# MLP up-projection by tokens with 512-wide moving weights, its inner layer turned by VectorE and through HBM

## The chip, the core and the metric

The kernel runs on one core of a Trainium2 chip. Five engines matter: TensorE (PE in the profile; PEld is its load of the still operand), VectorE (DVE), ScalarE (ACT), GpSimd (POOL) and SyncE (SP), which here only issues transfers. Each engine works through its own list in order and waits on semaphores for the others. The metric is the device time of one execution in microseconds (us); before the change its median is 823.63 us over three runs (823.33 to 824.06).

## What is computed

The reference is a trunk of two layers: a mixer with three attention-like branches, and then an MLP, each behind an RMS norm. Only the MLP is touched (x is 256 tokens by 1024, the inner layer has 4096 columns):

```python
def rms_norm(x, g, eps=NORM_EPS):
    xf = x.astype(jnp.float32)
    y = xf * lax.rsqrt(jnp.mean(xf * xf, axis=-1, keepdims=True) + eps)
    return (y * g.astype(jnp.float32)).astype(x.dtype)

def squared_relu_mlp(h, w_up, w_down):
    return jnp.square(jax.nn.relu(h @ w_up)) @ w_down

# in each of the two layers, behind the mixer:
h = rms_norm(x, mlp_norm[l])
x = x + squared_relu_mlp(h, w_mlp_up[l], w_mlp_down[l])
```

## The kernel before, in words

Every product is made from two parts: an operand is split into hi (rounded to the matmul's float32r) and lo (the rest), and hi*hi + hi*lo + lo*hi are summed in PSUM. A matmul is written `matmul(out, still, moving)`: the still operand (128 x 128) is loaded first, then up to 512 columns of the other move through.

*Weights.* `weight_plan` (L52) lays the weights out in HBM in the order of their use, in blocks of at most 128 x 1024 floats (512 KB). `load_w` takes the next block; `fetch` (L199) loads it into one of 7 `raw` buffers by a DMA on SP's queue (L195), ScalarE rounds it to `whi` (L210), VectorE subtracts to get `wlo` (L212). There are 6 buffers each of whi and wlo; the list of every engine is set by a scheduler ahead of the run.

*The normed input* `xm` (class Normed) lies turned, 1024 channels on partitions in 8 chunks k, 256 tokens along the row, as hi and lo side by side (`xs`). The gain is multiplied in. The factor 1/rms of each token is not: `stats` (L309) turns the sums of squares (`sqsum`, added by GpSimd at L288) on PE, VectorE sums them and GpSimd takes the power (L343), which gives a column of factors by token; `stats_row` (L348) turns that column on PE into a row.

*Up* (L1157 to L1175). One block f is 128 inner columns for all 1024 channels. The weights are still, the tokens move: for each of 8 chunks a matmul with whi against hi and lo of x together (512 columns, L1172), and for each chunk one with wlo against hi (256 columns, L1174). The result `pup` has inner columns on partitions and is already turned for the next product. The very last block of layer 1 takes another form, three 256-wide matmuls for each chunk (`project_t`, with `three`, L231 to L233).

*squared_relu* (L1177), for each block: ScalarE copies the hi*lo half out of PSUM (L1180), VectorE adds the other half (L1181), takes the maximum with 0 and multiplies with the row of factors (L1182), ScalarE squares (L1183), and `split_plain` (L252) makes hi and lo, `sq`.

*Down* (L1188). For each f, 2 halves of the tokens times 2 halves of the output columns, three matmuls of 512 columns each, with sq still and weights moving: 12 matmuls into four sums `acc` that stay in PSUM for the whole MLP. Up and down alternate in pairs: up f, f+1, then down f-2, f-1. The last 2 (layer 0) or 4 (layer 1) downs run in an order written out by hand, so that the four sums end one after the other. In layer 1, x itself is added into the sums by transposes on PE (`x_rows`, L1203).

Of the kernel before, what the change touches and what calls it, by code (L numbers as in the profile page):

```python
# [7 lines left out]
F32 = mybir.dt.float32  # L8
F32R = mybir.dt.float32r
# [5 lines left out]
P = 128  # L15
D = 1024
S = 256
# [3 lines left out]
DFF = 4096  # L21
NF = DFF // P

ENDS, WHOLE = [2] * (L - 1) + [4], [0] * (L - 1) + [1]
EPS = 1e-6
GN_EPS = 1e-5
NEG_INF = -1e30
# [19 lines left out]
    [c + 64 * h + i for h in range(8) for i in (*range(8), *range(16, 40), *range(8, 16), *range(40, 64))] for c in (416, 928)  # L47
)
C_KV = [P * h + o + i for o in (0, NOPE) for h in range(MLA_H) for i in range(64)]


def weight_plan():  # L52

    plan = []

    def block(key, name, kt, cols, per):
        for j in range(0, kt, per):
            plan.append(((*key, j // per), name, (j, per), cols))

    def turned(key, cols):  # L60
        for n in range(4):
            block((*key, n), "w_in", KD, cols[P * n : P * n + P], KD)

    def span(c, n):
        return range(c, c + n)

    for l in range(L):
        if l == 0:

            for i in range(2):  # L70
                plan.append(((l, "mq", i), "w_in", (0, 1), C_MQ[256 * i : 256 * i + 256]))
            plan.append(((l, "b0", 0), "w_in", (0, 1), C_MLA))
            for k in range(1, KD):
                plan.append(((l, "b0mq", k), "w_in", (k, 1), [*C_MLA, *C_MQ]))
        else:
            block((l, "b0"), "w_in", KD, C_MLA, 2)
            turned((l, "mq"), C_MQ)
        turned((l, "mk"), C_MK)
        block((l, "mv"), "w_in", KD, C_MV, 2)
        mv, plan = plan[-4:], plan[:-4]  # L80
        for i, (key, name, kt, cols) in enumerate(
            (("qrope", "mla_w_q_up", 2, C_QROPE), ("qnope", "mla_w_q_up", 2, C_QNOPE), ("kvup", "mla_w_kv_up", 1, C_KV))
        ):
# [12 lines left out]
        for i in range(2):  # L96
            block((l, "bmoba%d" % i), "w_branch_moba", 4, span(512 * i, 512), 2)
        for i in range(2):
            block((l, "gret%d" % i), "w_in", KD, span(C_GRET + 512 * i, 512), 2)
        for i in range(2):  # L100
            block((l, "bret%d" % i), "w_branch_ret", 4, span(512 * i, 512), 2)
        for n in range(KD):
            block((l, "wout", n), "w_out", KD, span(P * n, P), KD)
        for f in range(0, NF + 2, 2):
            for i in (f, f + 1) if f < NF else ():
                block((l, "up", i), "w_mlp_up", KD, span(P * i, P), KD)
            for i in (f - 2, f - 1) if 2 <= f <= NF - ENDS[l] else ():
                plan.append(((l, "down", i, 0), "w_mlp_down", (i, 1), range(D)))
        for i in range(NF - ENDS[l], NF):
            plan.append(((l, "down", i, 0), "w_mlp_down", (i, 1), range(D)))  # L110
    at, offset = {}, 0
    for key, name, (j, n), cols in plan:
        at[key] = (offset, n, len(cols))
        offset += P * n * len(cols)
    return plan, at, offset
# [22 lines left out]
def trunk(ctx: ExitStack, tc: tile.TileContext, gx, wts, consts, gfin, gn, xtok, out):  # L138
# [6 lines left out]
    wp = ctx.enter_context(tc.tile_pool(name="wp", bufs=1))  # L145
    sb = ctx.enter_context(tc.tile_pool(name="sb", bufs=1))
    ps = ctx.enter_context(tc.tile_pool(name="ps", bufs=1, space=bass.MemoryType.PSUM))


    GX = cp.tile([P, G_END + 4 * S], F32, name="GX")  # L150
# [20 lines left out]
    def load_w(*key):  # L171

        ahead = 0 if key[:2] in ((0, "b0"), (0, "mq"), (0, "b0mq")) else AHEAD
        have(min(ahead + 1, len(loaded) + len(order)))
        return loaded.pop(key)
# [45 lines left out]
    def misc_tile(name="misc"):  # L221
        return ps.tile([P, 512], F32, name=name, tag="misc", bufs=4)
# [156 lines left out]
    def project_t(l, key, n, xn, o):  # L379

        wh, wl = load_w(l, key, n, 0)
        for k in range(KD):
            xh, xl = xn.k(k)
            three(o, wh[:, k, :], wl[:, k, :], xh, xl, k == 0, k == KD - 1)
# [326 lines left out]
    def layer(l, xn, before):  # L711
# [442 lines left out]

        accs = [acc_tile() for _ in range(4)]

        def up(fs, between=None):  # L1157

            us = [misc_tile("pup") for _ in fs]
            if fs[0] >= NF - WHOLE[l]:
                project_t(l, "up", fs[0], xm, us[0][:, 0:S])
                return us
            ws = [load_w(l, "up", f, 0) for f in fs]
            jobs = [(part, i, k) for part in range(2) for i in range(len(fs)) for k in range(KD)]
            for part, i, k in sorted(jobs, key=lambda job: job[2]) if fs[0] == 0 else jobs:
                u, w = us[i], ws[i][part][:, k, :]
                if part == 0:
                    if between and k in between:  # L1170
                        between[k]()
                    nc.tensor.matmul(u, w, xm.both(k), start=k == 0, stop=False)  # L1172
                else:
                    nc.tensor.matmul(u[:, 0:S], w, xm.k(k)[0], start=False, stop=k == KD - 1)  # L1174
            return us  # L1175

        def squared_relu(f, u):  # L1177
            s = sb.tile([P, S], F32, name="relu", bufs=3)
            if f < NF - WHOLE[l]:
                nc.scalar.copy(s, u[:, S : 2 * S])  # L1180
                nc.vector.tensor_add(s, u[:, 0:S], s)  # L1181
            nc.vector.scalar_tensor_tensor(s, s if f < NF - WHOLE[l] else u[:, 0:S], 0.0, xm.row, op0=ALU.max, op1=ALU.mult)  # L1182
            nc.scalar.activation(s, s, AF.Square)  # L1183
            both = sb.tile([P, 2, S], F32R, name="sq", tag="w2k", bufs=W2K)
            latest[:] = split_plain(s, both[:, 0, :], both[:, 1, :])
            return both[:, 0, :], both[:, 1, :]

        def down(w, h2, t, half, f):  # L1188

# [16 lines left out]
                )  # L1206

        if last:
            gf = sb.tile([P, 2, D], F32, name="gf", tag="KK", bufs=1)
            nc.sync.dma_start(gf[:, 0, :], bass.AP(tensor=gfin.tensor, offset=gfin.offset, ap=[[0, P], [1, D]]))  # L1210

        latest, h2, first_end = [], {}, NF - ENDS[l]
        us = up([0]) + up([1], {4: lambda: xm.stats(accs[3])}) + up([2], {4: xm.stats_row}) + up([3])
        for f in range(0, NF, 2):
            if f >= 4:
                us = up([f, f + 1]) if f + 1 < NF - WHOLE[l] else up([f]) + up([f + 1])
            for i in range(2):
                h2[f + i] = squared_relu(f + i, us[i])
            us = us[2:]
            if last and f == 2:  # L1220
                for q in quarters:
                    x_rows(*q)
            for g in (f - 2, f - 1) if 2 <= f <= first_end else ():
                w = load_w(l, "down", g, 0)
                for q in quarters:
                    down(w, h2[g], *q, g)
        ws = [load_w(l, "down", f, 0) for f in range(first_end, NF)]
        order_pe = ExitStack()
        order_pe.enter_context(tc.manual_schedule(engines={mybir.EngineType.PE}))
# [58 lines left out]
        for t in range(NT):  # L1288
            y = sb.tile([P, D], F32, name="y", tag="t4", bufs=T4)
            r = sb.tile([P, 1], F32, name="fr", tag="st", bufs=SMALL)  # L1290
            s0, s1, s2 = (st[:, 3 * t + i : 3 * t + i + 1] for i in range(3))
            for half in range(2):
                cs = slice(512 * half, 512 * half + 512)
                ends[2 * t + half]()
                acc = accs[2 * t + half]
                square(acc, 3 * t + half)
                if half:
                    nc.vector.scalar_tensor_tensor(s2, s0, EPS, s1, op0=ALU.add, op1=ALU.add)
                    nc.gpsimd.tensor_tensor(r, s2, neghalf[:, 0:1], op=ALU.pow)
                nc.vector.tensor_mul(y[:, cs], acc, gf[:, 0, cs])  # L1300
            cs = slice(0, 320)
            nc.scalar.activation(y[:, cs], y[:, cs], AF.Copy, scale=r)
            nc.scalar.dma_start(out[:, t, cs], y[:, cs])
            cs = slice(320, D)
            nc.vector.tensor_scalar(y[:, cs], y[:, cs], r, None, op0=ALU.mult)
            nc.sync.dma_start(out[:, t, cs], y[:, cs])
# [112 lines left out]
```

## Time and profile before

| | |
|---|---|
| median of 3 runs | 823.63 us (823.33 to 824.06) |
| the profiled execution | 823.49 us |
| its span in the trace | 821.7 us |
| MLP of layer 0 in the span | about 233 to 409 us |
| MLP of layer 1 in the span | about 638 to 816 us |
| matmuls of up: 512 wide / 256 wide | 504 x 390 ns / 504 x 283 ns |
| DMA engines busy, whole span | 58.8% in the queue of SP and ScalarE |

Three things help in reading the profile. Matmuls overlap, so the mean duration of one (390 ns) is not the pace: the pace is the distance of two starts. A group of instructions is named by line, engine and operation, then `out<-in`; idle time is given with the engine that ended it. And the chain of work that ended last is followed back from the end; what isn't in it doesn't set the time.

The groups of squared_relu, from the view by line and form (busy us, mean ns of one, then idle time before it and what ended it):

```profile
L1180 ACT COPY relu<-pup 128x256 f32<-128x256 f32 x63 | 22.7, 365 | 15.5 <-PE pup L1174 15.4
L1181 DVE TENSOR_TENSOR relu<-pup,relu 128x256 f32<-128x256 f32 x63 | 26.0, 416 | 0.9 <-ACT relu L1180 0.9
L1182 DVE SCALAR_TENSOR_TENSOR relu<-relu,rrow 128x256 f32<-128x256 f32 x63 | 23.7, 415 | 1.4 <-ACT rrow L337 1.3
L1183 ACT ACTIVATE relu<-relu 128x256 f32<-128x256 f32 x64 | 25.5, 409 | 52.9 <-DVE relu L1182 52.9
```

### The profile page before, as it was taken

To read this page: it belongs to the slowest core of one execution; us is meant where nothing else is said; L and a number is where in the kernel's file an instruction comes from. 1 tells how busy PE (TensorE), PEld (TensorE's weight loads), DVE (VectorE), ACT (ScalarE), POOL (GpSimd) and SP (SyncE) were. 2 spreads that over 40 slices of the span, in tenths; PEclk is the share of its full clock that TensorE was granted. 3 is DMA by queue.
4 is the path that set the end of the run, shared out by engine and by line. 5 is a ranking of instruction groups with operands and counts; after the bars stand their busy time and mean duration, and the time that the engine had idled before them with its cause. 6 is when DMAs were issued, how large, how long until landed. Compare 5 with 4: busy or idle time off the path is not lost.

```text
span 821.7 us, 12140 instructions
## 1 busy us (share of the span) xinstructions
PE 815.1 (99%) x4291; PEld 694.1 (84%) x4291; DVE 600.6 (73%) x1083; ACT 473.2 (58%) x837; POOL 99.2 (12%) x75
## 2 busy tenths in 40 slices
PE   9999999999999999999999999999999999999997
PEld 7888888888888888888898888888888888888886
DVE  6879599797787566666697976887978766655663
ACT  7676655545566555555686566554546555555552
POOL 0100540330030000000035210013101200000000
PEclk9999999999999999999999999999999999999999
DMA  9974765856456665555457548548575666666611
GB/s 333 347 234 132 251 212 165 281 178 229 151 178 210 204 190 194 184 199 170 173 185 226 166 131 329 177 108 301 165 223 162 200 199 188 182 198 195 189 52 52
DMA packets 51133, 161.23 MB, mean 196 GB/s; under 512 B 7424, under 2 KB 11904, under 8 KB 50816
## 3 DMA queue, kind: packets, MB, share of 16 engines
q1 hardware_dynamic: 49728, 158.99, 58.8%
q10 hardware_dynamic: 1344, 1.46, 0.6%
q8 instruction: 34, 0.56, 0.3%
q14 instruction: 27, 0.22, 0.1%
HBM read 150.98 MB, written 1.05 MB: 185 GB/s over the span
## 4 chain that ended last, share of the span: by engine, by line
PE 99%; DVE 0%; ACT 0%; issue 0%; DVEq 0%
PE acc L231 18%; PE acc L233 18%; PE acc L232 18%; PE pup L1172 14%; PE pup L1174 7%; PE acc L1122 5%; PE acc L412 5%; PE acc L414 2%; PE ps_s L938 1%; PE acc L780 1%; PE po L579 1%; PE ps_s L481 1%; PE warm L691 0%; PE acc L782 0%; PE po L581 0%; PE pmt L1088 0%
## 5 line engine op out<-in xcount | busy, mean ns | idle before, releaser
L212 DVE TENSOR_TENSOR wlo<-raw,whi 128x1024 fp32r<-128x1024 f32 (+4 forms) x287 | 346.0, 1216 | 165.3 <-ACT whi L210 106.3
L210 ACT ACTIVATE whi<-raw 128x1024 fp32r<-128x1024 f32 (+4 forms) x287 | 290.8, 1023 | 178.6 <-PE acc L233 85.1
L1172 PE MATMUL pup<-xs,whi 128*128 128x512 f32 x504 | 123.5, 390 | 0.0
L231 PE MATMUL acc<-whi,xs 128*128 128x512 f32 (+1 forms) x304 | 118.7, 392 | 0.0
L233 PE MATMUL acc<-whi,xs 128*128 128x512 f32 (+1 forms) x304 | 118.4, 390 | 0.0
L232 PE MATMUL acc<-wlo,xs 128*128 128x512 f32 (+1 forms) x304 | 117.8, 387 | 0.0
L1172 PEld LDWEIGHTS pup<-xs,whi 128*128 128x128 f32 x504 | 93.4, 188 | 18.6
L231 PE MATMUL acc<-whi,sq 128*128 128x512 f32 x256 | 100.1, 391 | 0.0
L232 PE MATMUL acc<-wlo,sq 128*128 128x512 f32 x256 | 99.9, 390 | 0.0
L233 PE MATMUL acc<-whi,sq 128*128 128x512 f32 x256 | 98.5, 389 | 0.0
L1174 PE MATMUL pup<-xs,wlo 128*128 128x256 f32 x504 | 69.6, 283 | 0.0
L1174 PEld LDWEIGHTS pup<-xs,wlo 128*128 128x128 f32 x504 | 66.6, 191 | 3.1
L233 PEld LDWEIGHTS acc<-whi,xs 128*128 128x128 f32 x304 | 57.1, 188 | 11.5
L231 PEld LDWEIGHTS acc<-whi,xs 128*128 128x128 f32 x304 | 57.0, 188 | 11.4 <-issue 0.7
L232 PEld LDWEIGHTS acc<-wlo,xs 128*128 128x128 f32 x304 | 57.1, 188 | 11.0
L233 PEld LDWEIGHTS acc<-whi,sq 128*128 128x128 f32 x256 | 48.0, 188 | 10.2
L1183 ACT ACTIVATE relu<-relu 128x256 f32<-128x256 f32 x64 | 25.5, 409 | 52.9 <-DVE relu L1182 52.9
L231 PEld LDWEIGHTS acc<-whi,sq 128*128 128x128 f32 x256 | 48.2, 188 | 9.2
L232 PEld LDWEIGHTS acc<-wlo,sq 128*128 128x128 f32 x256 | 48.2, 188 | 8.9
L288 POOL TENSOR_TENSOR sqsum<-sqsum,xsq 128x256 f32<-128x256 f32 x16 | 16.7, 1046 | 281.1 <-ACT xs L247 169.8
L503 ACT ACTIVATE prob<-prob,smx 128x128 f32<-128x128 f32 x64 | 28.4, 445 | 26.0 <-DVE smx L500 26.0
L412 PE MATMUL acc<-xs,whi 128*128 128x512 f32 x160 | 40.5, 395 | 0.0
(227 smaller groups left out, 1125.2 us busy)
## 6 DMA issues: line engine op xcount, KB each, us to landing
raw<-wts SPq DMA_DIRECT2D x264, 512.0 KB, 4.3
probT<-blocks SPq DMA_DIRECT2D x80, 48.0 KB, 2.0
qkoth<-qkraw SPq DMA_DIRECT2D x48, 64.0 KB, 2.4
raw<-wts SPq DMA_DIRECT2D x5, 464.0 KB, 6.7
dec<-consts SPq DMA_DIRECT2D x2, 1024.0 KB, 6.4
raw<-wts SPq DMA_DIRECT2D x4, 416.0 KB, 3.2
raw<-wts SPq DMA_DIRECT2D x4, 256.0 KB, 4.2
xrow<-xtok SPq DMA_DIRECT2D x4, 256.0 KB, 7.2
```

Of the source, the lines that this page charges most:

```text
L210: nc.scalar.activation(hi[:, cs], raw[:, cs], AF.Copy)
L212: nc.vector.tensor_sub(lo[:, cs], raw[:, cs], hi[:, cs].bitcast(F32))
L231: nc.tensor.matmul(o, ah, bh, start=start, stop=False)
L232: nc.tensor.matmul(o, ah, bl, start=False, stop=False)
L233: nc.tensor.matmul(o, al, bh, start=False, stop=stop)
L288: (nc.gpsimd if n < self.on_pool else nc.vector).tensor_add(self.sum, self.sum, sq)
L412: nc.tensor.matmul(acc, wh[:, k, :], xn.both(k), start=k == 0, stop=False)
L503: nc.scalar.activation(p[:, a:b], p[:, a:b], AF.Exp, bias=m[:, 2 + i : 3 + i], scale=scale, accum_out=m[:, 4 + i : 5 + i])
L1122: nc.tensor.matmul(o, a, b, start=half == 0 and i == 0, stop=4 * half + n == KD and i == len(jobs) - 1)
L1172: nc.tensor.matmul(u, w, xm.both(k), start=k == 0, stop=False)
L1174: nc.tensor.matmul(u[:, 0:S], w, xm.k(k)[0], start=False, stop=k == KD - 1)
L1183: nc.scalar.activation(s, s, AF.Square)
```

## The change

Up is now computed by tokens: the tokens' hi and lo are still and the weights move, 512 inner columns at a time. A block of weights ("up", g, j) holds 2 chunks of channels for the 512 columns of group g; four such blocks make a group, with two sums in PSUM, one for each half of the tokens. 32 blocks of 12 matmuls make the 8 groups of a layer. Since tokens are now on partitions, the factor 1/rms is a column and goes into ScalarE's relu as its scale, and `stats_row` is not called in the MLP any more. The inner layer then has to be turned for down. VectorE transposes it in blocks of 32 by 32; one store of 512 KB takes the blocks to a buffer in HBM (`hbounce`), and four loads of 32 partitions each bring them back in changed places (`hturned`). ScalarE and VectorE split a whole group at once. The order is ten ups first (`LEAD`), then down i and up 10 + i in turn, and ten downs at the end. Buffers: the blocks and the turned group take slots of tags that the attention uses before (probT, t4), the split ones those of Q and KK; gf, the final norm's gain, moves to t4.

```diff
+LEAD = 10
+def mlp_order():
+
+    order = [("up", i) for i in range(LEAD)]
+    for i in range(NF):
+        order += [("down", i), ("up", LEAD + i)] if LEAD + i < NF else [("down", i)]
+    return order
...
+        for kind, i in mlp_order():
+            if kind == "up":
+                g, j = divmod(i, 4)
+                plan.append(((l, "up", g, j), "w_mlp_up", (2 * j, 2), span(512 * g, 512)))
+            else:
                 plan.append(((l, "down", i, 0), "w_mlp_down", (i, 1), range(D)))
...
-            us = [misc_tile("pup") for _ in fs]
-            if fs[0] >= NF - WHOLE[l]:
-                project_t(l, "up", fs[0], xm, us[0][:, 0:S])
-                return us
-            ws = [load_w(l, "up", f, 0) for f in fs]
...
-                    nc.tensor.matmul(u, w, xm.both(k), start=k == 0, stop=False)
-                else:
-                    nc.tensor.matmul(u[:, 0:S], w, xm.k(k)[0], start=False, stop=k == KD - 1)
...
+        def up(i):
+
+            g, j = divmod(i, 4)
+            if j == 0:
+                us[g] = [misc_tile("pup") for _ in range(NT)]
+            wh, wl = load_w(l, "up", g, j)
+            for kk in range(2):
+                k = 2 * j + kk
+                ah, al = xm.k(k)
+                for t in range(NT):
+                    sl = slice(P * t, P * t + P)
+                    three(us[g][t], ah[:, sl], al[:, sl], wh[:, kk, :], wl[:, kk, :], k == 0, k == KD - 1)
+            if i == 1:
+                xm.stats(accs[3])
+            if j == 3:
+                squared_relu(g)
+
+        def squared_relu(g):
+
+            blocks = sb.tile([P, 4 * S], F32, name="hblocks", tag="probT", bufs=2)
+            for t in range(NT):
+                s = w2k("relu")
+                nc.scalar.activation(s, us[g][t], AF.Relu, scale=xm.col[t])
+                nc.scalar.activation(s, s, AF.Square)
+                nc.vector.transpose(blocks.rearrange("p (b j t e) -> p t j b e", b=4, j=4, t=2)[:, t], s)
+            bounce = dr.tile([P, 4 * S], F32, name="hbounce", bufs=2)
+            nc.sync.dma_start(bounce, blocks)
+            turned = sb.tile([P, 4 * S], F32, name="hturned", tag="t4", bufs=T4)
+            for b in range(4):
+                src = bounce.rearrange("(a p) (b r) -> b p a r", a=4, b=4)[b]
+                nc.sync.dma_start(turned[32 * b : 32 * b + 32, :].rearrange("p (a r) -> p a r", a=4), src)
+            sq = sb.tile([P, 2, 4, S], F32R, name="sq", tag=("Q", "KK")[g % 2], bufs=1)
+            src = turned.rearrange("p (a m e) -> p m a e", a=4, e=32)
+            dst = (sq[:, i].rearrange("p j (t a e) -> p (j t) a e", a=4, e=32) for i in range(2))
+            latest[:] = split_plain(src, *dst)
+            for j in range(4):
+                h2[4 * g + j] = sq[:, 0, j, :], sq[:, 1, j, :]
...
-        us = up([0]) + up([1], {4: lambda: xm.stats(accs[3])}) + up([2], {4: xm.stats_row}) + up([3])
...
+        for kind, i in mlp_order()[: -ENDS[l]]:
+            if kind == "up":
+                up(i)
+                if last and i == LEAD - 1:
+                    for q in quarters:
+                        x_rows(*q)
+            else:
+                w = load_w(l, "down", i, 0)
                 for q in quarters:
-                    down(w, h2[g], *q, g)
+                    down(w, h2[i], *q, i)
```

The lists of the engines show what moves. Line numbers shift by 9 (L231 to L233 of `three` become L240 to L242, the load of weights L195 becomes L204, whi's rounding L210 becomes L219).

TensorE in the steady part of layer 0, before: the two ups of a pair, wide and narrow (xs with four numbers are the four tiles of the input, two chunks each).

```order
L1172 MATMUL pup<-xs_2228,whi 128x512 x2
L1172 MATMUL pup<-xs_2229,whi 128x512 x2
L1172 MATMUL pup<-xs_2230,whi 128x512 x2
L1172 MATMUL pup<-xs_2231,whi 128x512 x2
L1174 MATMUL pup<-xs_2228,wlo 128x256 x2
L1174 MATMUL pup<-xs_2229,wlo 128x256 x2
L1174 MATMUL pup<-xs_2230,wlo 128x256 x2
L1174 MATMUL pup<-xs_2231,wlo 128x256 x2
```

TensorE at the same stage of the changed kernel: the end of a down and the first half of the up behind it.

```order
L240 MATMUL acc_2499<-whi_2880,sq_2690 128x512
L241 MATMUL acc_2499<-wlo_2881,sq_2690 128x512
L242 MATMUL acc_2499<-whi_2880,sq_2690 128x512
L240 MATMUL pup_2840<-whi_2898,xs2_2232 128x512
L241 MATMUL pup_2840<-wlo_2899,xs2_2232 128x512
L242 MATMUL pup_2840<-whi_2898,xs2_2232 128x512
L240 MATMUL pup_2841<-whi_2898,xs2_2232 128x512
L241 MATMUL pup_2841<-wlo_2899,xs2_2232 128x512
L242 MATMUL pup_2841<-whi_2898,xs2_2232 128x512
```

All matmuls of up and down are now 512 wide, and one block of up (12 matmuls) stands between two of down, in place of 32 matmuls of up and 24 of down in turn.

SP's queue in layer 0, at the first two groups of the changed kernel; before, weight loads alone stand there. A row's waits stand in brackets (DMAHW are transfers, each of eight semaphores in turn).

```order
L1194 DMA hbounce<-hblocks 128x1024 [waits DVE_49]
L204 DMA raw<-wts 128x1024 [waits DMAHW4_49,DVE_49]
L1198 DMA hturned<-hbounce 32x4x256 [waits DMAHW5_49,DMAHW3_49,PE_49]
L1198 DMA hturned<-hbounce 32x4x256 [waits DMAHW6_49]
L1198 DMA hturned<-hbounce 32x4x256 [waits DMAHW7_49]
L1198 DMA hturned<-hbounce 32x4x256 [waits DMAHW0_49]
L204 DMA raw<-wts 128x1024 [waits DMAHW1_49,DVE_49]
L204 DMA raw<-wts 128x1024 [waits DMAHW2_49,DVE_49]
L204 DMA raw<-wts 128x1024 [waits DVE_49]
L1194 DMA hbounce<-hblocks 128x1024 [waits DMAHW4_49,DVE_49]
```

The store waits for the transposes and the first load back for the store; the loads of weights stand behind both in the same queue.

ScalarE in layer 0, from the split of group 0 to that of group 1, in the changed kernel:

```order
L261 ACTIVATE sq_2597<-hturned_2592 128x1024
L1190 ACTIVATE relu_2675<-pup_2600,ms_2540 128x512
L1190 ACTIVATE relu_2679<-pup_2601,ms_2540 128x512
L219 ACTIVATE whi_2769<-raw_2767 128x1024
L1191 ACTIVATE relu_2675<-relu_2675 128x512
L1191 ACTIVATE relu_2679<-relu_2679 128x512
L219 ACTIVATE whi_2787<-raw_2785 128x1024
L219 ACTIVATE whi_2824<-raw_2822 128x1024
L219 ACTIVATE whi_2844<-raw_2842 128x1024
L219 ACTIVATE whi_2862<-raw_2860 128x1024
L261 ACTIVATE sq_2690<-hturned_2685 128x1024
```

The split of a group waits for its four loads, and the relu of the next group and the rounding of weights stand behind it.

More of the change, by code (lines that the diff above doesn't have):

```diff
@@ L22 @@
 NF = DFF // P
-ENDS, WHOLE = [2] * (L - 1) + [4], [0] * (L - 1) + [1]
+ENDS = [2] * (L - 1) + [4]
+LEAD = 10
 EPS = 1e-6
@@ L103, in weight_plan @@
             block((l, "wout", n), "w_out", KD, span(P * n, P), KD)
[L104 to L107, printed above, removed]
+        for kind, i in mlp_order():
[3 more added lines that the diff above has]
+            else:
                 plan.append(((l, "down", i, 0), "w_mlp_down", (i, 1), range(D)))
-        for i in range(NF - ENDS[l], NF):
-            plan.append(((l, "down", i, 0), "w_mlp_down", (i, 1), range(D)))
     at, offset = {}, 0
@@ L147, in trunk @@
     ps = ctx.enter_context(tc.tile_pool(name="ps", bufs=1, space=bass.MemoryType.PSUM))
+    dr = ctx.enter_context(tc.tile_pool(name="dr", bufs=1, space=bass.MemoryType.DRAM))
     GX = cp.tile([P, G_END + 4 * S], F32, name="GX")
@@ L1155, in layer @@
         accs = [acc_tile() for _ in range(4)]
-        def up(fs, between=None):
-            us = [misc_tile("pup") for _ in fs]
-            if fs[0] >= NF - WHOLE[l]:
-                project_t(l, "up", fs[0], xm, us[0][:, 0:S])
-                return us
-            ws = [load_w(l, "up", f, 0) for f in fs]
[L1166 to L1172, printed above, removed]
-                else:
-                    nc.tensor.matmul(u[:, 0:S], w, xm.k(k)[0], start=False, stop=k == KD - 1)
-            return us
@@ L1177, in squared_relu @@
[L1177 to L1186, printed above, removed]
+        us, h2, latest = {}, {}, []
@@ L1208, in layer @@
         if last:
-            gf = sb.tile([P, 2, D], F32, name="gf", tag="KK", bufs=1)
-            nc.sync.dma_start(gf[:, 0, :], bass.AP(tensor=gfin.tensor, offset=gfin.offset, ap=[[0, P], [1, D]]))
-        latest, h2, first_end = [], {}, NF - ENDS[l]
-        us = up([0]) + up([1], {4: lambda: xm.stats(accs[3])}) + up([2], {4: xm.stats_row}) + up([3])
[L1214 to L1220, printed above, removed]
-                for q in quarters:
[L1222 to L1225, printed above, removed]
-                    down(w, h2[g], *q, g)
+            gf = sb.tile([P, D], F32, name="gf", tag="t4", bufs=T4)
+            nc.sync.dma_start(gf, bass.AP(tensor=gfin.tensor, offset=gfin.offset, ap=[[0, P], [1, D]]))
+        first_end = NF - ENDS[l]
+        for kind, i in mlp_order()[: -ENDS[l]]:
[6 more added lines that the diff above has]
+                w = load_w(l, "down", i, 0)
+                for q in quarters:
+                    down(w, h2[i], *q, i)
         ws = [load_w(l, "down", f, 0) for f in range(first_end, NF)]
@@ L1299, in layer @@
                     nc.gpsimd.tensor_tensor(r, s2, neghalf[:, 0:1], op=ALU.pow)
-                nc.vector.tensor_mul(y[:, cs], acc, gf[:, 0, cs])
+                nc.vector.tensor_mul(y[:, cs], acc, gf[:, cs])
             cs = slice(0, 320)
```

## The prediction

> **What bounds the kernel now.** I read the page from the top: span and busy time, then the chain that ended last, then the two MLP stretches in the view by windows.
>
> ```profile
> span 821.7 us, 12140 instructions
> PE   815.1 (99%) x4291; PEld 694.1 (84%) x4291; DVE 600.6 (73%) x1083; ACT 473.2 (58%) x837; POOL 99.2 (12%) x75
> PE 99%; DVE 0%; ACT 0%; issue 0%; DVEq 0%
> ```
>
> The first line has the span, the second the engines' busy time, the third the chain by engine: 99% of what sets the end is PE. The execution took 823.49 us, so 1.8 us lie outside the span; its time is 0.14 us below the median of the three runs (823.63). A measurement here can tell about 0.2% (1.65 us) from no change.
>
> ```profile
> core 0: us, PE busy (x) PEld busy (x) DVE busy (x) ACT busy (x) POOL busy (x), PEclk, DMA share, GB/s
> 252.00:405.00 153.00, 153.00 (x769) 130.56 (x768) 95.93 (x143) 85.16 (x144) 0.00 (x0) 1.00 0.58 189
> 658.00:816.00 158.00, 157.89 (x801) 134.76 (x799) 94.92 (x144) 84.52 (x144) 0.55 (x1) 1.00 0.52 159
> ```
>
> These windows are the two MLPs without their first 20 us. PE is busy in every microsecond at the full granted clock (1.00). VectorE, ScalarE and the DMA engines have a third or more to spare. A busy PE could still hide a slow pace, so the next view is the chain in order of time: start, length, line, count.
>
> ```profile
> 271.04 3.63 PE pup L1172 x16
> 274.67 1.91 PE pup L1174 x16
> ...
> 282.05 3.63 PE pup L1172 x16
> 285.68 1.91 PE pup L1174 x16
> ...
> 392.12 3.63 PE pup L1172 x16
> ```
>
> L1172 is the 512-wide matmul of the up-projection, L1174 the 256-wide one. One period holds two blocks f: 16 wide, 16 narrow, and 24 matmuls of down between them and the next pair. Eleven periods run from 271.04 to 392.12: 11.007 us each. A wide one takes 3.63/16 = 0.2267 us, a narrow one 1.91/16 = 0.1194 us, though half a wide one is 0.1134. **The narrow form carries about 6 ns too much each**; that is what the change can take.
>
> **The change, part by part.**
>
> *Wide for narrow.* The new up keeps tokens still and moves 512 weight columns. This shape, xs still and whi or wlo moving, already runs in the gates:
>
> ```profile
> 173.87 0.39 PE L231 MATMUL acc<-whi,xs 128*128 128x512 f32 x1
> ...
> 179.99 0.39 PE L231 MATMUL acc<-whi,xs 128*128 128x512 f32 x1
> ```
>
> There are 27 matmuls between these starts: 6.12/27 = 0.2267 us. A pair of old blocks moves 16x512 + 16x256 columns, which are 24 x 512, so columns are equal; a new period has 24 + 24 wide matmuls, 48 x 0.2267 = 10.88 us against 11.007, **0.127 us less**. Of this 16 x 6 ns = 0.10 is the narrow form, the rest the slower first matmuls where narrow turns to wide. Layer 0 has 16 pairs: 2.03 us. Layer 1 has 15: 1.90 us, and its last pair is of another form:
>
> ```profile
> 799.17 1.98 PE L1172 MATMUL pup<-xs,whi 128*128 128x512 f32 x8
> ...
> 804.82 0.40 PE L231 MATMUL acc<-whi,sq 128*128 128x512 f32 x1
> ```
>
> 5.65 us become 24 x 0.2267 = 5.44: 0.21 us.
>
> *stats_row leaves the MLP.* The norm's factor is now a column, given to ScalarE as a scale; the two turning matmuls at L348 go.
>
> ```profile
> 245.93 0.38 PE L348 MATMUL acc<-K,ms 128*128 128x128 f32 x2
> 246.06 2.10 PE L1172 MATMUL pup<-xs,whi 128*128 128x512 f32 x8
> ...
> 248.95 2.00 PE L1172 MATMUL pup<-xs,whi 128*128 128x512 f32 x8
> ```
>
> They hold PE 0.13 us, and the eight behind them take 2.10 instead of 2.00: 0.23 a layer, 0.46 in all. **Sum: 2.03 + 1.90 + 0.21 + 0.46 = 4.6 us less on PE, if nothing new stops it.**
>
> [...]
>
> *The activation.* It was three operations on each of ScalarE and VectorE for each 256-wide block; it becomes, for each group of four blocks, two relu, two squares and a split on ScalarE, two block transposes and a subtraction on VectorE.
>
> ```profile
> L513 DVE STREAM_TRANSPOSE blocks<-prob 128x384 f32<-128x384 f32 x24 | 12.5, 555 | 0.8 <-DMA probT<-blocks 0.8
> L615 ACT ACTIVATE th<-acc,half 128x512 f32<-128x512 f32 x24 | 15.7, 680 | 4.6 <-PE acc L233 4.6
> L210 ACT ACTIVATE whi<-raw 128x1024 fp32r<-128x1024 f32 x264 | 277.2, 1058 | 173.4 <-PE acc L233 83.9 <-PE pup L1172 44.6 <-issue 14.3
> L212 DVE TENSOR_TENSOR wlo<-raw,whi 128x1024 fp32r<-128x1024 f32 x264 | 330.8, 1262 | 160.1 <-ACT whi L210 103.5 <-PE pup L1174 52.9 <-PE acc L232 3.3
> ```
>
> From these rows, by size, a group costs ScalarE 4 x 0.68 + 1.06 = 3.8 us, VectorE 2 x 0.75 + 1.26 = 2.8 us in each 21.8 us (8 x 2.72, four ups and four downs). I cost it at nothing: both engines idle over a third of the windows above. Read in runs of 32, transpose output and subtraction could be slower; even double they fit.
>
> *The trip through HBM* is the one new wait. A group goes out as 512 KB and back as four reads of 128 KB. No such round trip is in the trace, so I bound its legs.
>
> ```profile
> DMA to landing us min/median/max: 2.5/2.6/2.7
> ...
> L195 SPq DMA_DIRECT2D raw<-wts x280: 327/328/1430, 1.2 to 783.2; - x140
> DMA to landing us min/median/max: 2.9/4.3/11.0
> ...
> L564 SPq DMA_DIRECT2D probT<-blocks x80: 512/589/1343, 73.8 to 552.7; - x80
> DMA to landing us min/median/max: 1.8/1.9/3.9
> ```
>
> From the view by line and by tile: the result's stores (the only writes to HBM) from issue to landing, then for the weight loads (512 KB) and for the 48 KB moves of probT first how long an issue holds SP (min/median/max in ns), then the landing. Out: 2.6 to 4.3 us. Back: four issues at 0.33 to 0.59, then 1.9 to 4.3: 3.2 to 6.7 us. I take the middle, 8.4 of 5.8 to 11.0, since weight loads share the engines.
>
> Who waits? In the steady part nobody on PE: six downs and six ups, 6 x 5.44 = 33 us, lie between a group's last up and its first down. The tight places are the first down and block 28.
>
> ```profile
> 232.78 1.55 PE L1172 MATMUL pup<-xs,whi 128*128 128x512 f32 x6
> ...
> 237.03 0.74 POOL L288 TENSOR_TENSOR sqsum<-sqsum,xsq 128x256 f32<-128x256 f32 x1 [1.61 <-ACT xsq L284]
> 242.50 1.62 POOL L343 TENSOR_TENSOR ms<-ms,neghalf 128x2 f32<-128x2 f32 x1 [4.73 <-DVE ms L342]
> ```
>
> *First down, layer 0.* wout ends at 232.8; six wide instead of three wide and three narrow stand ahead of it, so 233.1. Of the 120 matmuls of ten ups 114 follow, with the statistics' two transposes: first down at 233.1 + 25.8 + 0.2 = 259.1. The factor is ready at 244.1 as before (group 0's last up ends at 242.8); relu and squares to 246.8, second transpose to 247.6, round trip to 253.4 to 258.6, split (1.06, then 1.26) to 255.8 to 260.9. PE wants the low half at 259.6, with its third matmul: slack 3.8 us to a stall of 1.3, in the middle 1.3 us to spare. Layer 1 puts 16 transposes of x, 1.5 us, between, and is safe.
>
> *Block 28.* Behind up 31 come only six downs, 6 x 2.72 = 16.3 us. ScalarE does relu, one weight split and the squares, VectorE one wlo and two transposes: out at 5.2 us, back at 11.0 to 16.2, low half at 13.3 to 18.5 against 16.8: between 3.5 us to spare and 1.7 lost, in each layer. I take no stall: the middle is 15.9, and by then the weight loads thin out.
>
> *SP's queue* has five new issues a group, and it stops twice: the store waits for the transposes, the reads for the store. Weight loads queue behind. Their ring is 7 deep: 7 x 2.72 = 19.0 us from issue to use, less 4.3 for landing leaves 14.7; SP stands still for up to 5.2 + 4.3 + 2.4 = 11.9. ScalarE's split of a group waits in order too, with weight splits behind it, but four or more blocks (10.9 us) are split ahead at that point. Traffic rises by 1 MB in 21.8 us, 48 GB/s on 189: 0.58 becomes 0.73 at the same efficiency.
>
> **The rivals.**
>
> *Stalls at the edges eat the gain.* All upper ends together: 1.3 + 2 x 1.7 = 4.7 us, so 823.6; half of it, 821.2. For it: the order lets the second bank's hi pass the first bank's low half at the first down, and loads are issued between store and reads. Against: the middles all fit.
>
> *Weights come late: slower.* If the store lands later than 14.7 - 5.2 - 2.4 = 7.1 us after issue, SP holds the weight stream longer than the ring covers, 16 times: at 7.8 us it costs 16 x 0.7 = 11 us, so 830. Against it: stores land in 2.6 us, although one load took 11.0. [...]
>
> *The change doesn't make PE faster.* If what stretches the narrow matmuls is the stream of weights or of results around them, and not their own form, the new wide ones pay it as well; then only stats_row's 0.46 us goes: 823.0. For it: the count of columns is the same. Against: the gates' 27 starts, with the same operands in the same places. [...]
>
> **How the numbers follow.** All hidden: 823.5 - 4.6 = 818.9 in this execution, **819.0** against the median; chance 0.66. Edge stalls, 820 to 823.6: 0.21. PE no faster: 0.05. Weights late: 0.08. The range begins at 818.2, as far below as the three runs lie apart (823.33 to 824.06), and goes to 822.6, over most of the edge stalls. Faster by over 0.2% (below 822.0) holds the first case and most of the second: 0.80; the rest of the second and the third make same 0.13; slower 0.07.
>
> **What would show it.** PE stays at 99% of a span of some 817 us with about 4,020 matmuls (264 and 4 fewer); pup and acc in L240 to L242 start 0.2267 us apart; no PE idle before the first down (about 26 us behind wout) or block 28; the store lands in 2.6 to 4.3 us and ScalarE's split of hturned ends before its down starts; SP's waits never reach whi. A gap before the first sq matmul would be the edge rival; whi waiting for DMA would be the slow one.

## The result, and the profile after

| | before | after |
|---|---|---|
| median, runs of one chip in turn | 823.48 us (823.13 to 824.06, 4 runs) | 819.32 us (818.90 to 819.60, 4 runs) |
| ratio to before | | 0.9948 (95% interval 0.9931 to 0.9966) |
| the profiled execution / its span | 823.49 / 821.7 us | 819.33 / 817.2 us |

The change makes the kernel about 4.2 us faster. First the head of the page of the changed kernel: span, busy time by engine, the chain by engine.

```profile
span 817.2 us, 11451 instructions
PE 810.5 (99%) x4023; PEld 679.8 (83%) x4023; DVE 573.4 (70%) x940; ACT 459.8 (56%) x724; POOL 97.1 (12%) x75
PE 99%; DVE 0%; ACT 0%; issue 0%; DVEq 0%
```

PE still sets the end, with 4,023 matmuls in place of 4,291: exactly the 264 and 4 that the change drops. All that PE waited for in the execution, from its view of waits (engine and tile, who ended it: us in total, times, longest):

```profile
PE warm L700 <- PEq L1426: 0.8, 1, 0.8
```

That is the warm-up; the MLP has no row. Next the windows of the two MLPs, columns as in the same view of before:

```profile
252.00:405.00 153.00, 153.00 (x678) 126.73 (x677) 83.70 (x79) 79.86 (x95) 0.00 (x0) 1.00 0.72 243
658.00:812.00 154.00, 153.23 (x685) 126.78 (x683) 80.81 (x79) 78.95 (x96) 0.55 (x1) 1.00 0.62 207
```

PE is busy for 153.0 of 153 us and 153.2 of 154, at a granted clock of 1.00. VectorE fell by 12 us and ScalarE by 5 in the first window, and the DMA engines went from 0.58 to 0.72 busy, for the trip through HBM. Now the first down of layer 0, from the timelines of PE, ScalarE and VectorE (start, duration):

```profile
259.24 0.39 PE L240 MATMUL acc<-whi,sq 128*128 128x512 f32 x1
...
259.92 0.39 PE L242 MATMUL acc<-whi,sq 128*128 128x512 f32 x1
```

```profile
256.47 1.06 ACT L261 ACTIVATE sq<-hturned 128x1024 fp32r<-128x1024 f32 x1 [4.13 <-DMA hturned<-hbounce]
```

```profile
257.56 1.23 DVE L261 TENSOR_TENSOR sq<-hturned,sq 128x1024 fp32r<-128x1024 f32 x1 [3.96 <-ACT sq L261]
```

The hi half is ready at 257.53 and the low half at 258.79; PE takes them at 259.24 and 259.92, so 1.7 and 1.1 us were to spare. Last the DMA issues of the page (number, size, median us from issue to landing):

```profile
raw<-wts SPq DMA_DIRECT2D x264, 512.0 KB, 4.6
hbounce<-hblocks SPq DMA_DIRECT2D x16, 512.0 KB, 4.5
hturned<-hbounce SPq DMA_DIRECT2D x64, 128.0 KB, 2.9
```

A store landed like a weight load of the same size, 4.5 us in the median against 4.6; the view by tile has 2.6, 4.5 and 6.2 us as its least, median and most.

### The profile page after: what moved, and what is told of

Read it like the earlier page. It is cut to its first block, busy times and chain, and to the rows that moved or that the text cites. A ratio compares the mean times of both kernels' runs of the same rounds, so it can differ in the third digit from the quotient of the medians.

```text
span 817.2 us, 11451 instructions
## 1 busy us (share of the span) xinstructions
PE 810.5 (99%) x4023; PEld 679.8 (83%) x4023; DVE 573.4 (70%) x940; ACT 459.8 (56%) x724; POOL 97.1 (12%) x75
## 3 DMA queue, kind: packets, MB, share of 16 engines
q10 hardware_dynamic: 1344, 1.46, 0.6%
## 4 chain that ended last, share of the span: by engine, by line
PE 99%; DVE 0%; ACT 0%; issue 0%; DVEq 0%
PE acc L242 18%; PE acc L240 18%; PE acc L241 18%; PE pup L241 7%; PE pup L242 7%; PE pup L240 7%; PE acc L1131 5%; PE acc L421 5%; PE acc L423 2%; PE ps_s L947 1%; PE acc L789 1%; PE po L588 1%; PE ps_s L490 1%; PE warm L700 0%; PE acc L791 0%; PE po L590 0%
## 5 line engine op out<-in xcount | busy, mean ns | idle before, releaser
L221 DVE TENSOR_TENSOR wlo<-raw,whi 128x1024 fp32r<-128x1024 f32 (+4 forms) x287 | 342.4, 1212 | 113.1 <-ACT whi L219 110.2
L219 ACT ACTIVATE whi<-raw 128x1024 fp32r<-128x1024 f32 (+4 forms) x287 | 287.6, 1022 | 168.3 <-PE acc L242 92.5
L240 PE MATMUL acc<-whi,xs 128*128 128x512 f32 (+1 forms) x304 | 118.7, 392 | 0.0
L242 PE MATMUL acc<-whi,xs 128*128 128x512 f32 (+1 forms) x304 | 118.4, 390 | 0.0
L240 PE MATMUL acc<-whi,sq 128*128 128x512 f32 x256 | 99.9, 390 | 0.0
L241 PE MATMUL pup<-wlo,xs 128*128 128x512 f32 x256 | 99.8, 390 | 0.0
L242 PE MATMUL pup<-whi,xs 128*128 128x512 f32 x256 | 99.6, 389 | 0.0
L242 PE MATMUL acc<-whi,sq 128*128 128x512 f32 x256 | 99.6, 389 | 0.0
L240 PE MATMUL pup<-whi,xs 128*128 128x512 f32 x256 | 99.3, 389 | 0.0
L261 DVE TENSOR_TENSOR sq<-hturned,sq 128x1024 fp32r<-128x1024 f32 x16 | 19.6, 1225 | 77.6 <-ACT sq L261 77.6
L242 PEld LDWEIGHTS acc<-whi,xs 128*128 128x128 f32 x304 | 57.1, 188 | 11.5
L240 PEld LDWEIGHTS acc<-whi,xs 128*128 128x128 f32 x304 | 57.0, 188 | 11.5 <-issue 0.7
L241 PEld LDWEIGHTS acc<-wlo,xs 128*128 128x128 f32 x304 | 57.1, 188 | 10.9
L261 ACT ACTIVATE sq<-hturned 128x1024 fp32r<-128x1024 f32 x16 | 17.0, 1061 | 80.9 <-DMA hturned<-hbounce 80.9
L240 PEld LDWEIGHTS acc<-whi,sq 128*128 128x128 f32 x256 | 48.1, 188 | 10.0
L242 PEld LDWEIGHTS acc<-whi,sq 128*128 128x128 f32 x256 | 48.0, 188 | 10.0
L242 PEld LDWEIGHTS pup<-whi,xs 128*128 128x128 f32 x256 | 48.1, 188 | 9.8
L241 PEld LDWEIGHTS pup<-wlo,xs 128*128 128x128 f32 x256 | 48.1, 188 | 9.8
L240 PEld LDWEIGHTS pup<-whi,xs 128*128 128x128 f32 x256 | 47.9, 188 | 9.8
```

The lines of the kernel that those rows point to most:

```text
L219: nc.scalar.activation(hi[:, cs], raw[:, cs], AF.Copy)
L221: nc.vector.tensor_sub(lo[:, cs], raw[:, cs], hi[:, cs].bitcast(F32))
L240: nc.tensor.matmul(o, ah, bh, start=start, stop=False)
L241: nc.tensor.matmul(o, ah, bl, start=False, stop=False)
L242: nc.tensor.matmul(o, al, bh, start=False, stop=stop)
L261: return nc.scalar.activation(hi, src, AF.Copy), nc.vector.tensor_sub(lo, src, hi.bitcast(F32))
```

## The experiments

All start from the changed kernel, whose 819.32 us and span of 817.2 are what they are set against. Two theories ran through them: that PE's matmuls alone set the time and the trip lies under them, and the rivals of the prediction, that the narrow form is not what cost the time, that the edges stall, or that the weights come late.

### Narrow matmuls again: halves, quarters, uneven pieces

`e1_halves` cuts every matmul of up in two of 256 columns; columns, products and operands stay.

```diff
-                    three(us[g][t], ah[:, sl], al[:, sl], wh[:, kk, :], wl[:, kk, :], k == 0, k == KD - 1)
+                    for c in range(2):
+                        cs = slice(256 * c, 256 * c + 256)
+                        three(us[g][t][:, cs], ah[:, sl], al[:, sl], wh[:, kk, cs], wl[:, kk, cs], ...)
```

> Each matmul of the new up is cut into two of 256 columns; same columns, 384 more matmuls a layer. If the narrow form itself costs 12 ns a pair (0.1194 us against half of 0.2267), a layer takes 768 x 0.1194 - 384 x 0.2267 = 4.6 us longer, and the turns between narrow and wide add up to 0.9 us: 819.3 + 9.3 to 11 = 828.6 to 830.4. [...]

Measured: 830.16 us (829.82 to 830.80, 4 runs), 10.8 more for 768 matmuls more: 14 ns each. With nothing else changed, the 256-wide form cost that time; its matmuls start 0.1196 us apart in this run.

`e2_quarters` does the same with four pieces of 128 (`range(4)`, `128 * c`).

> The same with four matmuls of 128 columns. If the time of a matmul is a fixed part and a part by columns, the two paces give 12 ns + 0.419 ns a column, 66 ns here: 1536 x 0.0657 - 384 x 0.2267 = 13.9 us a layer, 847 in all. If the narrow pace of 0.119 us is a floor set by the load of the still operand, 1536 x 0.119 = 183 us a layer: over 1000 us. [...]

Measured: 990.01 us (989.79 to 990.57, 4 runs). PE's timeline in the steady part of this run:

```profile
300.02 0.28 PE L241 MATMUL pup<-wlo,xs 128*128 128x128 f32 x1
300.13 0.27 PE L242 MATMUL pup<-whi,xs 128*128 128x128 f32 x1
300.25 0.28 PE L240 MATMUL pup<-whi,xs 128*128 128x128 f32 x1
...
300.58 0.27 PE L240 MATMUL pup<-whi,xs 128*128 128x128 f32 x1
300.69 0.28 PE L241 MATMUL pup<-wlo,xs 128*128 128x128 f32 x1
```

Six starts lie 0.67 us apart, 0.112 each, for a quarter of the columns of a matmul that takes 0.2267. So an up matmul of 128 columns took only 0.008 us less than one of 256, at 0.1196 in the run with halves: a floor, as it seems, and 256 stands just above it. Neither expectation gave this time, but the pace does: 1536 x 0.112 less 384 x 0.2267 is 85 us a layer, 989 in all. PEld has one load of 0.19 us for each matmul, started 0.11 us after the one before.

`e9_uneven` asks whether that floor is one of each matmul or of the loads on average: 384 and 128 columns in turn.

```diff
+                    for m, (a, w) in enumerate(((ah, wh), (ah, wl), (al, wh))):
+                        for c, cs in enumerate((slice(0, 384), slice(384, 512))):
+                            nc.tensor.matmul(us[g][t][:, cs], a[:, sl], w[:, kk, cs], ...)
```

> Each wide matmul of up becomes one of 384 and one of 128 columns, in turn: 768 of each, columns and products as before. From 512 wide (0.2267 us) and 256 wide (0.1196 in the run with halves) a matmul costs 0.418 ns a column and 12.5 ns, so 384 takes 0.173; the run with quarters showed 0.112 where this line gives 0.066 for 128. Theory A, the 0.112 is a floor of every single matmul (its own load of the still operand can't be hidden behind a short neighbour): the two take 0.285, 768 x 0.058 = 45 us more, 864. Theory B, the floor is one of the loads on average, and a long matmul gives the load behind it time: 0.173 + 0.066 = 0.239, 768 x 0.0125 = 9.6 us more, 829. Theory C, the 12.5 ns aren't a cost of every matmul but the edge of the floor, felt at 256 alone: 384 takes 0.170, and with A's floor it is 862, with B's 822 or less.

Measured: 866.41 us (2 runs within 0.01). PE's timeline, merged by equal instructions (x4 is two pairs):

```profile
374.92 0.45 PE L1181 MATMUL pup<-wlo,xs 128*128 128x384 f32 x2
375.20 0.74 PE L1181 MATMUL pup<-whi,xs 128*128 128x384 f32 x4
...
377.50 0.45 PE L1181 MATMUL pup<-wlo,xs 128*128 128x384 f32 x2
```

Nine pairs in 2.58 us are 0.287 each, where theory A wanted 0.285 and theory B 0.239. B is out: 384 columns beside them didn't pay for the 128. The starts of PEld's loads in this run lie 0.11 and 0.18 us apart in turn (300.62 to 300.91 us holds one of each). In the stretches read, of this run and of the one with quarters (both from 300 to 302 us), no load of up starts sooner than 0.11 us after the one before it, while a matmul of 384 columns starts 0.06 us after the one of 128 ahead of it (300.62 and 300.68). So the floor of these runs is seen between loads, not between matmuls; what makes it is not shown. Whether the 256-wide form pays a fixed 12 ns or the edge of this floor (theory C, 862) is not told apart by 2 us in 47.

### The trip left out, and doubled

`e3_no_trip` leaves the store and the four loads out; the split reads the blocks as VectorE left them, so the inner layer's blocks are not in their places and the result is another.

```diff
-            bounce = dr.tile([P, 4 * S], F32, name="hbounce", bufs=2)
-            nc.sync.dma_start(bounce, blocks)
...
+            turned = blocks
```

> The store to HBM and the four loads back are left out; the split reads the transposed blocks where they lie (the inner layer's blocks are not put in their places). If the trip is hidden altogether, 819.3 as before it (818.8 to 819.8) and a span of 817.2. If it costs something by stalls or by its traffic, shorter by that: 818 or less.

Measured: 818.72 us (818.41 to 819.02, 4 runs), 0.6 below the changed kernel. Where the 0.6 lies is told by PE's timeline around layer 0's MLP: the end of wout ahead of it and the first yd matmul behind it. First this run, then the changed kernel:

```profile
231.69 1.12 PE L1131 MATMUL acc<-mT,wlo 128*128 128x256 f32 x8
...
402.93 0.60 PE L1270 MATMUL pyd<-K,ydn 128*128 128x128 f32 x4
```

```profile
232.16 1.12 PE L1131 MATMUL acc<-mT,wlo 128*128 128x256 f32 x8
...
403.40 0.60 PE L1275 MATMUL pyd<-K,ydn 128*128 128x128 f32 x4
```

Between the two rows lie 171.24 us in both. In layer 1, from the end of wout to the last matmul of down, it is 174.54 us in both. The difference is ahead of the first MLP, 231.69 against 232.16, where the kernels are the same; the other runs with the same code there have 231.6 to 232.8 at this row, so it is not the trip's. **The trip costs nothing.**

`e8_two_trips` sends each group out and back a second time, in one store and one load on the same queue.

```diff
+            again = dr.tile([P, 4 * S], F32, name="hagain", bufs=2)
+            nc.sync.dma_start(again, turned)
+            turned = sb.tile([P, 4 * S], F32, name="hturned2", tag="t4", bufs=T4)
+            nc.sync.dma_start(turned, again)
```

> A second store to HBM and load back behind the first, for every group. A store and a load take some 7 us more. If only the edges feel the trip, the four places stall by 6 + 4 + 6 + 5 us less what the order hides, 835 to 841, and between them PE stays dense. If SP's standing still makes the weights late, it now stands still for about 14 of the 14.7 us that the ring of raw covers, so at the most a few us more, seen as rounding to whi waiting for DMA. If all is hidden, 819.3.

Measured: 868.67 us (866.50 to 871.71, 4 runs), far above what was expected. PE's waits:

```profile
PE acc L240 <- ACT sq L261: 29.6, 5, 9.1
PE acc L241 <- DVE wlo L221: 3.8, 4, 1.0
PE acc L240 <- ACT whi L219: 1.4, 2, 1.2
```

30 us are stalls for ScalarE's split at five places, only 5 are for weights; the rest of the 52.7 us in the span is PE itself, busy for 828.1 us instead of 810.5 at a mean clock of 0.978. Both were unexpected, and the next runs take them apart.

`e11_two_trips_lead12` has the two trips and `LEAD = 12`.

> Two trips for each group as before (868.7, with 35 us of PE waits, 30 of them for ScalarE's split), but twelve ups ahead, so each group has 5.4 us more until its first down. If the wait is that of the groups at the edges: those of 3.9 at the first down and 4.9 at block 24 go, 9.2, 5.9 and 5.8 at the last groups shrink by 5.4 or go, and with each the spell of half clock behind it: 820 to 832, PE waits under 8 us. If instead SP's queue holds the weight stream up, twelve ups ahead change nothing in it: above 850, with waits for whi and wlo in place of sq.

Measured: 859.09 us (858.88 to 859.29, 2 runs). That is the time of the second theory, but half of the waits are still for the split, so neither theory holds as it stands. PE's waits, then ScalarE's own longest:

```profile
PE acc L240 <- ACT sq L261: 12.3, 2, 8.3
PE acc L240 <- ACT whi L219: 8.0, 4, 3.2
PE acc L241 <- DVE wlo L221: 5.2, 7, 1.0
```

```profile
ACT sq L261 <- DMA hturned<-hagain: 160.1, 16, 15.6
```

The waits for the split shrank from 30 to 13 us, but the weights, 5.2 us late before, are now 13.2 us late. The second row suggests why: ScalarE stands at the split, up to 15.6 us. Its timeline at such a place (idle time ahead in brackets) and PE's:

```profile
364.05 1.06 ACT L261 ACTIVATE sq<-hturned 128x1024 fp32r<-128x1024 f32 x1 [14.46 <-DMA hturned<-hagain]
365.02 1.04 ACT L219 ACTIVATE whi<-raw 128x1024 fp32r<-128x1024 f32 x1
```

```profile
366.11 0.49 PE L240 MATMUL acc<-whi,sq 128*128 128x512 f32 x1 [2.01 <-ACT whi L219]
```

The rounding of the next weights comes right behind the split that waited 14.46 us, and PE starts when it ends. In layer 0 all five waits for weights, of eleven in the run, come within 3.6 us behind the start of a split for which ScalarE had stood 12.8 us or more, and there is none where it stood 11.7 or less; ScalarE itself waited for raw weights once in that MLP, for 1.65 us. SP's queue could still be to blame as well, since it stands for both trips too.

`e12_pool_split` decides: the same kernel with the split on GpSimd, which has nothing else queued there.

```diff
-            latest[:] = split_plain(src, *dst)
+            hi, lo = dst
+            latest[:] = nc.gpsimd.tensor_copy(hi, src), nc.gpsimd.tensor_sub(lo, src, hi.bitcast(F32))
```

> Two trips and twelve ups ahead as in the run before (859.1; PE waits 26 us: 12.3 for the split, 13.2 for whi and wlo), but the split of a turned group is made by GpSimd alone, which has nothing else to do there; ScalarE and VectorE no longer wait for the trip. Theory A, the weights came late because their rounding stands behind ScalarE's split in its list (it stood up to 14.5 us, four blocks cover 10.9): the waits for whi and wlo fall from 13.2 to under 2 us, though SP's queue is as before. Theory B, they came late because SP's queue stood for the trips: these waits stay at 10 us or more, and ScalarE then waits for raw. The waits for the split itself grow by what GpSimd is slower (its 128x256 took 0.74, so some 6 us a group instead of 2.3), so the time can't be told from this beforehand: 835 to 860; the waits decide.

Measured: 823.08 us (820.43 to 825.95, 8 runs), 36 less than with the split on ScalarE and VectorE, and 3.7 more than one trip takes with twelve ups ahead (819.37, below). PE's waits and SP's, whose queue still stands for the trips (its three rows are the waits of the loads for the store, of the second store, and of the second load):

```profile
PE acc L240 <- POOL sq L1207: 2.5, 2, 1.6
PE acc L242 <- POOL sq L1207: 1.7, 2, 1.2
```

```profile
SPq L1198 <- DMA hbounce<-hblocks: 55.0, 16, 7.8
SPq L1200 <- DMA hturned<-hbounce: 39.7, 27, 3.6
SPq L1202 <- DMA hagain<-hturned: 33.2, 16, 3.7
```

Not one wait for weights is left, though SP waited for the trips as long as before (55.0 + 39.7 + 33.2 = 128 us against 49.1 + 37.0 + 34.0 = 120 in the run before). **What made weights late for PE was that the split stood ahead of their rounding in the lists of ScalarE and VectorE, not SP's queue and not the traffic.** The edit moves both halves of the split, so it doesn't tell the two lists apart. SP's queue may not be harmless either: in this run ScalarE waited 14.1 us for raw weights in all, up to 4.6 at a time, against 7.5 and 1.7 in the run before; PE still had enough rounded ones.

### The lead: 12, 9 and 8 blocks ahead

Each of these changes the one line `LEAD = 10`.

> Two more ups ahead, so 5.4 us more slack at both places. If nothing stalls in the changed kernel, 819.3 (818.8 to 819.8); if it still loses time at the edges that the trace doesn't show, 818 or less.

> One up fewer ahead of the first down, and one down fewer behind the last up. In the changed kernel's trace the low half of the first group is ready 1.1 us before its matmul in layer 0 and 3 us in layer 1, that of the last group 1.0 and 2.2 us. If these slacks are real, taking 2.72 us from each costs 1.6 + 0 + 1.7 + 0.5, some 3 to 4 us: 822 to 823.5. If the trip isn't near the edge, 819.3.

> Two fewer: with the same slacks 4.3 + 2.4 + 4.4 + 3.2 = 14 us of stall at most, 831 to 834; if PE finds other work ahead of the waiting down, less. If the trip isn't near the edge, 819.3.

Measured, 4 runs each: 819.37 us (819.09 to 819.76) with 12, 819.88 (818.78 to 820.60) with 9, 829.50 (827.01 to 830.70) with 8. With 12 nothing is gained, so the change has no edge stall left to remove. With 9 the expected 3 to 4 us aren't there: PE's waits have only the warm-up. Layer 0 takes the same 170.28 us from the end of wout to the first yd matmul as with ten, and layer 1 takes 0.43 more, at a wait for the low half of 0.11 us at 662.70, too short for that view. PE's timeline of layer 0 shows why. The first down starts at 259.05 us, not 2.7 before the 259.24 of ten ups, since the scheduler filled in matmuls of the tenth up; and at block 28 it put the eight products that need hi alone ahead of the four with the low half. Besides, the slack of the last group was read too small ahead of these runs, 1.0 and 2.2 us: with ten the first matmul that takes its low half starts at 395.92 and 800.64, 2.2 and 3.2 us behind it. With 8 the stall comes. PE's timeline in layer 0, at block 28:

```profile
394.93 0.39 PE L242 MATMUL acc<-whi,sq 128*128 128x512 f32 x1
398.60 0.79 PE L240 MATMUL acc<-whi,sq 128*128 128x512 f32 x1 [3.28 <-ACT sq L261]
399.19 0.63 PE L241 MATMUL acc<-wlo,sq 128*128 128x512 f32 x1
399.62 0.63 PE L240 MATMUL acc<-whi,sq 128*128 128x512 f32 x1
400.04 0.63 PE L241 MATMUL acc<-wlo,sq 128*128 128x512 f32 x1
```

PE waits 3.28 us, and then the starts lie 0.425 us apart instead of 0.227, up to 404.31; behind the stall of layer 1 they lie as far apart from 811.10 to 814.09. The windows around both show the granted clock (the 0.72 and the 0.83, ahead of the DMA share):

```profile
398.00:410.00 12.00, 11.40 (x39) 9.14 (x40) 4.21 (x4) 3.79 (x6) 0.00 (x0) 0.72 0.36 131
808.00:818.00 10.00, 8.53 (x29) 6.64 (x30) 2.09 (x4) 2.26 (x5) 0.00 (x0) 0.83 0.00 0
```

In layer 0 the 14 matmuls from 398.60 to 404.71 took 6.1 us, where 14 x 0.2267 is 3.2. In all PE waits 5.7 us in the MLPs and is busy 816.0 us instead of 810.5: here the stalls are paid about twice. With the two trips 35.1 us of waits came with 17.6 us more of busy time, half as much again.

### Turning on PE, and stats_row put back

`e4_pe_turn` turns the inner layer by eight transposes on PE for a group, with no trip.

```diff
-                nc.vector.transpose(blocks.rearrange("p (b j t e) -> p t j b e", b=4, j=4, t=2)[:, t], s)
...
+            for half in range(2):
+                pt = misc_tile("pht")
+                for jj in range(2):
+                    for t in range(NT):
+                        c = P * (2 * jj + t)
+                        j = 2 * half + jj
+                        nc.tensor.transpose(pt[:, c : c + P], s2[t][:, P * j : P * j + P], ident)
+                dst = (sq[:, i, 2 * half : 2 * half + 2].rearrange("p j s -> p (j s)") for i in range(2))
+                latest[:] = split_plain(pt, *dst)
```

> The group is turned by 8 transposes of 128 x 128 on TensorE instead of by VectorE and HBM. If PE sets the end, the 64 transposes a layer are paid in full: 16 transposes of x hold PE 1.66 us, so 6.6 us a layer and some 0.1 us a group for the refill: 819.3 + 14 to 15 = 833 to 834.5. If PE had room, the time would stay at 819 to 821.

Measured: 838.91 us (837.91 to 839.32, 4 runs), 19.6 more, and 4.4 above the expected range. The transposes cost what was expected: PE is busy for 825.4 us, 14.9 more for 128 of them (0.116 each with what they do to the matmul behind). What was not expected is that PE waits where it didn't:

```profile
PE pht L1200 <- ACT relu L1191: 3.9, 2, 2.8
```

With the turn on PE the up-projection by tokens is 15.4 us slower than the kernel before; it is worth having only with the turn off PE.

`e10_stats_row` puts the two matmuls back behind the third up.

```diff
+            if i == 2:
+                xm.stats_row()
```

> The two matmuls that turn the factor into a row, which nobody needs now, are put back behind the third block of up in both layers. By the prediction 0.23 us a layer, 0.46 in all: 819.8, and in the trace the time from wout's end to the first yd matmul of layer 0 goes from 170.3 to 170.5. If they cost nothing: 819.3 and 170.3. The median can hardly tell it, the trace can.

Measured: 819.52 us (818.91 to 820.86, 5 runs), which alone says nothing. In its trace wout ends at 232.60 and the first yd matmul starts at 403.12: 170.52 us against 170.28 in the changed kernel, 0.24 more; the runs with nine, ten and twelve ups ahead and without the trip agree in this stretch to 0.01. In layer 1, from the end of wout to the last matmul of down, it is 174.77 against 174.54.

## Why the prediction was right, step by step

**PE sets the end, and the new period is 48 wide matmuls.** Shown by the waits, the windows and the count. The rows at the two ends of layer 0's MLP, the first matmul behind wout and the first yd matmul, before and then after:

```profile
232.78 1.55 PE L1172 MATMUL pup<-xs,whi 128*128 128x512 f32 x6
...
405.69 0.60 PE L1261 MATMUL pyd<-K,ydn 128*128 128x128 f32 x4
```

```profile
233.12 0.40 PE L240 MATMUL pup<-whi,xs 128*128 128x512 f32 x1
...
403.40 0.60 PE L1275 MATMUL pyd<-K,ydn 128*128 128x128 f32 x4
```

The stretch took 172.91 us before and 170.28 after. Part of that only moves: after, six wide matmuls of up stand ahead of wout's end in place of three wide and three narrow, and wout ends 0.34 later, where the prediction put it (233.1). So the layer wins 2.29 us where the prediction summed 2.03 + 0.23 = 2.26. Layer 1, from the end of wout to the last matmul of down, went from 177.24 to 174.54; less the 0.33 by which the end of wout moves there too, it wins 2.37 where the prediction summed 2.34. Behind the last matmul the tail grew by 0.14 (6.20 to 6.34), and the span fell by 4.5 of the predicted 4.6.

**The narrow form carries about 6 ns too much.** The size was right. Cutting wide ones in two cost 14 ns a pair, where twice the 6 ns that the prediction read from the old kernel is 12. Not shown is what the 6 ns are; up's matmuls of 128 columns took 0.112 us, and the 256-wide ones of the old kernel, at 0.1194, only 7 ns more.

**stats_row: 0.23 us a layer.** 0.24 and 0.23 by its own run.

**The activation costs nothing.** Both engines' busy time fell in the window, as shown. From the view by line and form, operations of the right size that the prediction had to guess:

```profile
L261 ACT ACTIVATE sq<-hturned 128x1024 fp32r<-128x1024 f32 x16 | 17.0, 1061 | 80.9 <-DMA hturned<-hbounce 80.9
L1192 DVE STREAM_TRANSPOSE hblocks<-relu 128x512 f32<-128x512 f32 x32 | 20.8, 687 | 0.9 <-ACT relu L1191 0.9
```

The transpose was costed at 0.75 us and took 0.69; the split, read in runs of 32, took about as long as a weight's: 1061 and 1225 ns on ScalarE and VectorE against 1056 and 1258.

**The trip, 5.8 to 11.0 us, taken as 8.4, and its slack.** At group 0 the store was issued at 247.21 and the last load had landed when the split began, 256.47: 9.3 us, 0.9 over the middle. Over all 16 groups the trip took 6.8 to 11.2 us with a median of 9.9, and stores landed as late as 6.2 us after their issue, where the prediction's bound was 4.3. So in the steady part the middle was 1.5 us too small, which cost nothing there; at block 28, where it counted, the trip took 8.0 and 6.8 us. The predicted 1.3 us to spare at the first down were 1.1, in part by luck: the store left 0.4 us earlier than summed and PE wanted the low half 0.3 later, against the 0.9 of the trip. At block 28 the low half came 15.2 us after its relu began in layer 0 (378.44 to 393.67) and 14.0 in layer 1, against a predicted middle of 15.9. The end of VectorE's half of that split in layer 0, and the first matmul that takes it:

```profile
392.45 1.22 DVE L261 TENSOR_TENSOR sq<-hturned,sq 128x1024 fp32r<-128x1024 f32 x1 [2.85 <-ACT sq L261]
```

```profile
395.92 0.39 PE L242 MATMUL acc<-whi,sq 128*128 128x512 f32 x1
```

The run with twelve ups ahead gave the same time, the run without the trip the same MLPs, and with two ups fewer the stall was there. So the edges were hidden, in layer 0 by 1.1 us at the first down and by 2.2 at block 28.

**The rivals.** *Edge stalls*: not there. Their price was mis-sized: the prediction counted idle time alone, 4.7 us for all upper ends, while behind the stall of 3.28 us with eight ups ahead the slower starts cost PE another 2.9 us. *Weights late*: not there, and its mechanism was named in the wrong place. The prediction put the point of decision into SP's queue, at a store landing 7.1 us after its issue; stores landed in at most 6.2. With two trips and the split on GpSimd SP stood for 128 us, against 47 in the changed kernel, without making a weight late for PE. What decided was how long ScalarE stands at the split, which the prediction mentioned as covered by four blocks or 10.9 us. It stood at most 8.8 us in the changed kernel, and 12.8 or more wherever PE waited for weights in layer 0 with two trips and twelve ups ahead. SP's stores took 4.5 us in the median, where the prediction set 2.6 against this rival. *PE no faster*: refuted by the layers' 2.29 and 2.37 us and by the halves.

## What to carry to other kernels

Where PE is the bound, count matmul instructions and not only columns: here 264 fewer for the same columns were worth 4 us, and any turn of data that this needs has to be done off PE, since the same turn on PE cost 19.6. A long trip for data can be hidden as long as the instruction that waits for it has nothing urgent behind it in its own engine's list (one trip cost nothing, two cost 3.7 us with the split on GpSimd and 40 with it on ScalarE and VectorE, with twelve ups ahead), so look there before blaming the queue of transfers. And leave slack at the places where PE could wait: a stall of a few us can be paid a second time in clock, as with eight ups ahead, where waits of 5.7 us came with 5.5 us more of busy time.

## What the runs showed of the hardware that was not expected

- An up matmul cut to 128 columns took 0.112 us, nearly what one of 256 did (0.1196), against 0.2267 for 512. One of 384 beside it didn't make up for that: 384 and 128 in turn took 0.287, with the loads of up's still operand 0.11 and 0.18 us apart.
- With eight ups ahead, the granted clock was 0.72 in the 12 us around a wait of PE of 3.28 us, with starts 0.425 us apart for 5.1 us, and 0.83 in the 10 us around two waits of 1.28 and 0.53 us in close succession, with such starts for 3.0 us. Yet by the same view it stayed at 1.00 around a single wait of 2.82 us in the run with PE's transposes (242 to 252 us), and around waits of 1.55 and 1.20 with the split on GpSimd (268 to 280 and 400 to 410 us). What makes one wait cost clock and another not is left open.
- With the split on GpSimd, VectorE's subtraction of weights took 1344 ns in the mean, in place of 1258 in the changed kernel; which of the edits between the two runs (lead, second trip, split) did it is not shown. GpSimd took 1.20 us to round 128 x 1024 values and 2.78 to subtract them.
